# Relu and row sum of a 16384 x 1024 array on one core: two row regions (111 and 17 rows per partition) in place of three (1, 111 and 16)

## The chip, the core and the metric

The kernel runs on one core of a Trainium2 chip. The metric is device time in microseconds (us): the median of repeated executions. Beside those stands one execution recorded by the profiler, whose span runs from the first instruction to the last.

## The reference

```python
def reference(x):                      # x: (32, 512, 1024) float32
    relu_x = np.maximum(x, 0)
    return np.sum(relu_x, axis=-1).astype(np.float32)    # (32, 512)
```

There are 32 x 512 = 16384 rows of 1024 numbers; each gives one sum of its positive numbers. The input is 67.1 MB, the output 64 KB.

## The kernel before, in words

**Layout.** The 16384 rows are dealt to 128 partitions, 128 rows to each. `REGIONS = [1, 111, 16]` cuts the input into three consecutive regions; in a region of n rows per partition, partition p owns n neighbouring rows, so that a load of several rows is one run of memory per partition (n x 4 KB). The sums are collected in `res`, one column per row of the partition (128 columns).

**Big chunks.** `CHUNKS` has seven entries (`NBIG = 7`) of 16 rows per partition, 8 MB each. Chunk 0 is two loads, one row of the first region and 15 of the second; chunks 1 to 6 are one load each. They go in turn into the three slots of `buf` (`NB = 3`). All loads are issued on SP, in one queue (line 91); from chunk 3 on SP waits (line 87, semaphore `s_dve`) until VectorE (DVE) has summed the chunk that held the slot. The two loads of chunk 0 are moved ahead of SP's drain at the start of the program (line 96), so that they are issued first of all.

**Work on chunks 0 to 5.** ScalarE (ACT) applies Relu in place in steps of several rows (`ACT_STEPS`, line 145), DVE follows with `tensor_reduce` over several rows at once (`DVE_STEPS`, line 160). In chunk 5 four rows are left out of this and done whole, two by ACT (line 127: Relu with an accumulated sum) and two by DVE (line 130: maximum with 0, accumulated). After chunk 1 DVE transposes the first 32 columns of `res` into `turned` (line 169, 32 x 32 blocks), so that the sums of the one-row region lie along 4 partitions, 32 in each.

**Chunk 6 and the tail.** The rows of chunk 6 are done whole and singly, by DVE and ACT in turn. The third region is loaded in shrinking pieces: 8, 4 and 2 rows (`TAIL`, line 101), each shared half and half, and the last two rows in column pieces (line 112): columns 0 to 912 of the first of them, then the last 512 of the second, then 256 to 512 of the second; the 112 + 256 columns in between go to `seam` (line 115). Each column piece gives a partial sum into a spare column of `seam`; at last ACT sums 114 and DVE 258 columns of `seam`, partial sums among them, and so the last two rows' sums are complete. The whole tail lies in slot `tb` = 1 of `buf`; SP issues its loads once chunk 4 has been summed.

**Stores.** Three, all on SP: `turned` (4 rows of 128 bytes, line 117, after semaphore `s_turn`); the 111 columns of the second region (444 bytes per partition, line 123, after chunk 6 is summed and the last load has landed); and the 16 columns of the tail (64 bytes per partition, line 207, after the last two sums). SP then waits for all stores to land (lines 208 and 209).

Of the kernel before, what the change touches and what calls it, by code (L numbers as in the profile page):

```python
# [3 lines left out]
P = 128  # L4
D = 1024
BIG = 16
NB = 3
REGIONS = [1, 111, 16]
CHUNKS = [[(0, 0, 1), (1, 0, 15)]] + [[(1, 16 * c + 15, 16)] for c in range(6)]
ACT_STEPS = [[16], [7, 9], [7, 9], [7, 9], [4, 5, 7], [3, 4, 5]]  # L10
DVE_STEPS = [[4, 5, 7], [7, 4, 5], [7, 4, 5], [7, 4, 5], [4, 5, 7], [3, 4, 5]]
TAIL = [8, 4, 2]
CUT = 912
HEAD = 256

# [1 line left out]
def bass_relu_sum_kernel(  # L17
    nc: bass.Bass,
    x: bass.AP,
    out: bass.AP,  # L20
):

    fp32 = mybir.dt.float32
    ALU = mybir.AluOpType
    AF = mybir.ActivationFunctionType
    X = mybir.AxisListType.X

    B, S, _ = x.shape
    J = B * S // P
    NBIG = len(CHUNKS)
    assert BIG * NBIG + sum(TAIL) + 2 == J == sum(REGIONS)  # L40

    xr = x.rearrange("b s d -> (b s) d")
    of = out.rearrange("b s -> (b s)")
    start = [sum(REGIONS[:i]) for i in range(len(REGIONS))]
    xv = [
        xr[P * s : P * (s + n), :].rearrange("(p j) d -> p j d", p=P)
        for s, n in zip(start, REGIONS)
    ]
    ov = [of[P * s : P * (s + n)].rearrange("(p j) -> p j", p=P) for s, n in zip(start, REGIONS)]

    buf = nc.alloc_sbuf_tensor("buf", [P, NB, BIG, D], fp32)
    w = D - CUT
    seam = nc.alloc_sbuf_tensor("seam", [P, 2 + w + HEAD + 2], fp32)
    res = nc.alloc_sbuf_tensor("res", [P, J], fp32)
    turned = nc.alloc_sbuf_tensor("turned", [P, 32], fp32)

    n_in = NBIG + len(TAIL) + 3
    s_in = [nc.alloc_semaphore(f"s_in{i}") for i in range(n_in)]
    s_act = nc.alloc_semaphore("s_act")
    s_dve = nc.alloc_semaphore("s_dve")  # L60
    s_fact = nc.alloc_semaphore("s_fact")
    s_fdve = nc.alloc_semaphore("s_fdve")
    s_half = nc.alloc_semaphore("s_half")
    s_seam = nc.alloc_semaphore("s_seam")
    s_last = nc.alloc_semaphore("s_last")
    s_turn = nc.alloc_semaphore("s_turn")
    s_store = nc.alloc_semaphore("s_store")
    s_out = nc.alloc_semaphore("s_out")

    sp, act, dve = nc.sync, nc.scalar, nc.vector  # L70

    NTWO = len(ACT_STEPS)
    done = [sum(map(len, DVE_STEPS[: c + 1])) for c in range(NTWO)]


    tb = NBIG % NB


    code = nc.main_func.blocks[0].instructions
    arrival = next(  # L80
        i
        for i, ins in enumerate(code)
        if ins.engine == mybir.EngineType.SP and type(ins).__name__ == "InstDrain"
    )
    for c in range(NBIG + 1):
        if c >= NB:
            sp.wait_ge(s_dve, done[c - NB])
        if c < NBIG:
            i = 0
            for g, j, n in CHUNKS[c]:  # L90
                sp.dma_start(  # L91
                    out=buf[:, c % NB, i : i + n, :], in_=xv[g][:, j : j + n, :]
                ).then_inc(s_in[c], 16)
                i += n
                if c == 0:
                    code.insert(arrival, code.pop())
                    arrival += 1
    r = 0
    tail = []
    for i, n in enumerate(TAIL):  # L100
        sp.dma_start(out=buf[:, tb, r : r + n, :], in_=xv[-1][:, r : r + n, :]).then_inc(  # L101
            s_in[NBIG + i], 16
        )
        tail.append((r, n, s_in[NBIG + i]))
        r += n


    rows = xv[-1].rearrange("p j d -> p (j d)")[:, r * D : (r + 2) * D]
    flat = buf[:, tb, r : r + 2, :].rearrange("p j d -> p (j d)")
    first, second, third = [(0, CUT), (D + D // 2, 2 * D), (D + HEAD, D + D // 2)]  # L110
    for k, (lo, hi) in enumerate((first, second, third)):
        sp.dma_start(out=flat[:, lo:hi], in_=rows[:, lo:hi]).then_inc(  # L112
            s_in[NBIG + len(TAIL) + k], 16
        )
    sp.dma_start(out=seam[:, 2 : 2 + w + HEAD], in_=rows[:, CUT : D + HEAD]).then_inc(s_seam, 16)
    sp.wait_ge(s_turn, 1)
    sp.dma_start(
        out=of[0:P].rearrange("(k q) -> k q", q=32), in_=turned[0:P:32, 0:32]
    ).then_inc(s_store, 16)
    sp.wait_ge(s_fact, 1)  # L120
    sp.wait_ge(s_fdve, 1)
    sp.wait_ge(s_in[-1], 16)
    sp.dma_start(out=ov[1][:, :], in_=res[:, start[1] : start[2]]).then_inc(s_store, 16)


    def on_act(t, acc):
        return act.activation(t, t, AF.Relu, accum_out=acc)  # L127

    def on_dve(t, acc):
        return dve.tensor_scalar(  # L130
            out=t, in0=t, scalar1=0.0, scalar2=None, op0=ALU.max, op1=ALU.add, accum_out=acc
        )

    def row(c, i):
        return buf[:, c % NB, i, :], res[:, c * BIG + i : c * BIG + i + 1]

    k = 0
    for c in range(NTWO):
        alone = BIG - sum(ACT_STEPS[c])
        act.wait_ge(s_in[c], 16 * len(CHUNKS[c]))  # L140
        r = 0
        ready = []
        for n in ACT_STEPS[c]:
            t = buf[:, c % NB, r : r + n, :]
            act.activation(t, t, AF.Relu).then_inc(s_act, 1)  # L145
            k += 1
            ready += [k] * n
            r += n
        for i in range(BIG - alone // 2, BIG):
            on_act(*row(c, i))  # L150
        if alone:
            dve.wait_ge(s_in[c], 16 * len(CHUNKS[c]))
            for i in range(BIG - alone, BIG - alone // 2):
                on_dve(*row(c, i))
        r = seen = 0
        for n in DVE_STEPS[c]:
            if ready[r + n - 1] > seen:
                seen = ready[r + n - 1]
                dve.wait_ge(s_act, seen)
            dve.tensor_reduce(  # L160
                out=res[:, c * BIG + r : c * BIG + r + n],
                in_=buf[:, c % NB, r : r + n, :],
                axis=X,
                op=ALU.add,
            ).then_inc(s_dve, 1)
            r += n
        if c == 1:
            dve.wait_ge(s_dve, done[c])
            dve.transpose(out=turned[:, :], in_=res[:, 0:32]).then_inc(s_turn, 1)  # L169


    j0 = NBIG * BIG
    for c in range(NTWO, NBIG):
        act.wait_ge(s_in[c], 16 * len(CHUNKS[c]))
        dve.wait_ge(s_in[c], 16 * len(CHUNKS[c]))
        for i in range(BIG):
            ins = (on_act if i % 2 else on_dve)(*row(c, i))
            if i >= BIG - 2:
                ins.then_inc(s_fact if i % 2 else s_fdve, 1)
    for r, n, s in tail:  # L180
        act.wait_ge(s, 16)
        dve.wait_ge(s, 16)
        for i in range(r, r + n):
            f = on_act if (i - r) % 2 else on_dve
            f(buf[:, tb, i, :], res[:, j0 + i : j0 + i + 1])

    lo, hi = first
    act.wait_ge(s_in[-3], 16)
    dve.wait_ge(s_in[-3], 16)
    on_act(flat[:, lo : CUT // 2], seam[:, 0:1]).then_inc(s_half, 1)  # L190
    on_dve(flat[:, CUT // 2 : hi], seam[:, 1:2]).then_inc(s_half, 1)
    k = 2 + w
    lo, hi = second
    act.wait_ge(s_in[-2], 16)
    on_act(flat[:, lo:hi], seam[:, k + HEAD : k + HEAD + 1]).then_inc(s_seam, 1)
    lo, hi = third
    dve.wait_ge(s_in[-1], 16)
    on_dve(flat[:, lo:hi], seam[:, k + HEAD + 1 : k + HEAD + 2]).then_inc(s_seam, 1)
    act.wait_ge(s_seam, 16 + 2)
    act.wait_ge(s_half, 2)  # L200
    on_act(seam[:, 0:k], res[:, J - 2 : J - 1]).then_inc(s_last, 1)
    dve.wait_ge(s_seam, 16 + 2)
    on_dve(seam[:, k : k + HEAD + 2], res[:, J - 1 : J]).then_inc(s_last, 1)


    sp.wait_ge(s_last, 2)
    sp.dma_start(out=ov[-1][:, :], in_=res[:, start[-1] : J]).then_inc(s_out, 16)
    sp.wait_ge(s_store, 16 * (len(REGIONS) - 1))
    sp.wait_ge(s_out, 16)
# [28 lines left out]
```

## Time and profile before

| | us |
|---|---|
| median of 3 runs | 160.85 (160.80 to 160.91) |
| span of the profiled execution, first to last instruction | 159.4 |
| what the median has beyond that span | 1.45 |
| DVE busy in the span | 120.6 |
| ACT busy in the span | 101.5 |

The profiled execution's own time is not recorded apart from its span, so the span stands for it. In the lines shown further down, a line of the timeline reads: start, duration, engine, source line, operation, what it writes and reads, how many instructions were merged, and in brackets the time that the engine sat idle ahead of it and what ended that. A line of the chain reads: start, duration, engine or DMA, tile and line. "SPq" is SP's queue; its durations are those of issuing.

### The profile page before, as it was taken

How to read it: one execution, taken by the hardware profiler on the slowest of the kernel's cores; microseconds unless marked ns; L12 is line 12 of the kernel's file. 1: busy time of each engine (PE TensorE's matmuls, PEld its weight loads, DVE VectorE, ACT ScalarE, POOL GpSimd, SP SyncE). 2: the span in 40 equal slices, each digit the busy share in tenths (PEclk: the TensorE clock that was granted, in tenths of full speed). 3: DMA queues.
4: the chain of work that ended last, by engine and by line, in shares of the span. 5: the costliest groups of instructions: out<-in, count | busy, mean ns of one | idle time of the engine just before them, and what ended most of it. 6: DMA issues, size and time to landing. Idle time of an engine off the chain costs nothing.

```text
span 159.4 us, 150 instructions
## 1 busy us (share of the span) xinstructions
DVE 120.6 (76%) x59; ACT 101.5 (64%) x54; POOL 0.2 (0%) x4
## 2 busy tenths in 40 slices
DVE  0000000009999999999999999999999999898995
ACT  3000059980799708996099941999329980496975
POOL 0000000000000000000000000000000000000000
DMA  9997996996996997989979969969969979798994
GB/s 378 493 401 339 493 526 263 526 526 263 526 493 296 526 444 345 526 378 411 526 312 477 526 263 526 526 263 526 526 263 526 444 345 526 321 469 374 417 400 142
DMA packets 2457, 67.18 MB, mean 421 GB/s; under 512 B 536, under 2 KB 792, under 8 KB 1176
## 3 DMA queue, kind: packets, MB, share of 16 engines
q1 hardware_dynamic: 2456, 67.18, 98.1%
q14 instruction: 1, 0.01, 0.0%
HBM read 67.11 MB, written 0.07 MB: 421 GB/s over the span
## 4 chain that ended last, share of the span: by engine, by line
DVE 55%; DMA 34%; ACT 9%; SPq 2%; issue 0%
DVE res L160 54%; DMA buf<-in_x_dram 34%; ACT buf L145 9%; SPq L101 1%; SPq L112 1%; DVE buf L130 0%; DVE seam L130 0%; SPq L91 0%; DVE turned L169 0%
## 5 line engine op out<-in xcount | busy, mean ns | idle before, releaser
L160 DVE TENSOR_REDUCE res<-buf 128x4 f32<-128x4096 f32 (+3 forms) x18 | 99.4, 5596 | 35.5 <-ACT buf L145 35.5
L145 ACT ACTIVATE buf<-buf 128x7168 f32<-128x7168 f32 (+5 forms) x13 | 80.4, 6233 | 46.1 <-DMA buf<-in_x_dram 46.1
L127 ACT ACTIVATE buf<-buf 128x1024 f32<-128x1024 f32 (+2 forms) x19 | 19.0, 999 | 8.9 <-DMA buf<-in_x_dram 8.9
L130 DVE TENSOR_SCALAR_CACHE_REDUCE buf<-buf 128x1024 f32<-128x1024 f32 (+2 forms) x19 | 20.7, 1143 | 1.7 <-DMA buf<-in_x_dram 1.6
L127 ACT ACTIVATION_READ_ACCUMULATOR buf<-buf 128x1 f32 x19 | 3.6, 188 | 0.0
L145 ACT ACT_TABLE_LOAD x1 | 1.3, 1283 | 1.3 <-PEq L223 1.3
L130 DVE DVE_READ_ACCUMULATOR buf<-buf 128x1 f32 x19 | 1.6, 84 | 0.0
L130 DVE TENSOR_SCALAR_CACHE_REDUCE seam<-seam 128x258 f32<-128x258 f32 x1 | 0.4, 421 | 0.0
L127 ACT ACTIVATE seam<-seam 128x114 f32<-128x114 f32 x1 | 0.3, 300 | 0.1
L169 DVE STREAM_TRANSPOSE turned<-res 128x32 f32<-128x32 f32 x1 | 0.2, 211 | 0.0
L127 ACT ACTIVATION_READ_ACCUMULATOR seam<-seam 128x1 f32 x1 | 0.2, 186 | 0.0
L223 POOL MEMSET const-bfloat16-1.0<- 128x1 bf16 x1 | 0.1, 101 | 0.0
L223 POOL MEMSET const-uint8-127<- 128x1 uint8 x1 | 0.1, 101 | 0.0
L223 POOL MEMSET const-float32-0.0<- 128x1 f32 x1 | 0.1, 98 | 0.2 <-issue 0.2
L223 POOL MEMSET const-float32-1.0<- 128x1 f32 x1 | 0.1, 98 | 0.0
L130 DVE DVE_READ_ACCUMULATOR seam<-seam 128x1 f32 x1 | 0.1, 82 | 0.0
## 6 DMA issues: line engine op xcount, KB each, us to landing
buf<-in_x_dram SPq DMA_DIRECT2D x1, 7680.0 KB, 21.1
buf<-in_x_dram SPq DMA_DIRECT2D x1, 4096.0 KB, 25.3
buf<-in_x_dram SPq DMA_DIRECT2D x1, 2048.0 KB, 29.9
buf<-in_x_dram SPq DMA_DIRECT2D x1, 1024.0 KB, 31.9
buf<-in_x_dram SPq DMA_DIRECT2D x1, 512.0 KB, 3.3
buf<-in_x_dram SPq DMA_DIRECT2D x1, 456.0 KB, 32.5
buf<-in_x_dram SPq DMA_DIRECT2D x1, 256.0 KB, 32.7
seam<-in_x_dram SPq DMA_DIRECT2D x1, 184.0 KB, 32.6
```

Of the source, the lines that this page charges most:

```text
L101: sp.dma_start(out=buf[:, tb, r : r + n, :], in_=xv[-1][:, r : r + n, :]).then_inc(s_in[NBIG + i], 16)
L112: sp.dma_start(out=flat[:, lo:hi], in_=rows[:, lo:hi]).then_inc(s_in[NBIG + len(TAIL) + k], 16)
L127: return act.activation(t, t, AF.Relu, accum_out=acc)
L130: return dve.tensor_scalar(out=t, in0=t, scalar1=0.0, scalar2=None, op0=ALU.max, op1=ALU.add, accum_out=acc)
L145: act.activation(t, t, AF.Relu).then_inc(s_act, 1)
L160: dve.tensor_reduce(out=res[:, c * BIG + r : c * BIG + r + n], in_=buf[:, c % NB, r : r + n, :], axis=X, op=ALU.add,).then_inc(s_dve, 1)
L169: dve.transpose(out=turned[:, :], in_=res[:, 0:32]).then_inc(s_turn, 1)
L223: nc = _bacc.Bacc("TRN2", target_bir_lowering=False, num_devices=1)
```

## The change

The input is cut into two regions of 111 and 17 rows per partition. Chunk 0 is one load of 15 rows; the row that the one-row region held comes in through the tail, whose first piece is 9 rows instead of 8. In that piece ACT now takes five rows and DVE four. The transpose on DVE, its tile, its semaphore and its store are gone. The last store has 17 columns (68 bytes per partition) instead of 16. The last two rows are loaded into a tile of their own, `ends`, as the tail slot's 16 rows would no longer hold 17 rows. Chunk 0's ACT step has 15 rows and its last DVE step 6 instead of 7; the columns of `res` shift with it (`col`).

```diff
-REGIONS = [1, 111, 16]
-CHUNKS = [[(0, 0, 1), (1, 0, 15)]] + [[(1, 16 * c + 15, 16)] for c in range(6)]
-ACT_STEPS = [[16], [7, 9], [7, 9], [7, 9], [4, 5, 7], [3, 4, 5]]
-DVE_STEPS = [[4, 5, 7], [7, 4, 5], [7, 4, 5], [7, 4, 5], [4, 5, 7], [3, 4, 5]]
-TAIL = [8, 4, 2]
+REGIONS = [111, 17]
+CHUNKS = [[(0, 15)]] + [[(16 * c + 15, 16)] for c in range(6)]
+ACT_STEPS = [[15], [7, 9], [7, 9], [7, 9], [4, 5, 7], [3, 4, 5]]
+DVE_STEPS = [[4, 5, 6], [7, 4, 5], [7, 4, 5], [7, 4, 5], [4, 5, 7], [3, 4, 5]]
+TAIL = [9, 4, 2]
...
-    turned = nc.alloc_sbuf_tensor("turned", [P, 32], fp32)
+    ends = nc.alloc_sbuf_tensor("ends", [P, 2 * D], fp32)
...
-            for g, j, n in CHUNKS[c]:
+            for j, n in CHUNKS[c]:
                 sp.dma_start(
-                    out=buf[:, c % NB, i : i + n, :], in_=xv[g][:, j : j + n, :]
+                    out=buf[:, c % NB, i : i + n, :], in_=xv[0][:, j : j + n, :]
                 ).then_inc(s_in[c], 16)
...
-    flat = buf[:, tb, r : r + 2, :].rearrange("p j d -> p (j d)")
+    flat = ends[:, :]
...
-    sp.wait_ge(s_turn, 1)
-    sp.dma_start(
-        out=of[0:P].rearrange("(k q) -> k q", q=32), in_=turned[0:P:32, 0:32]
-    ).then_inc(s_store, 16)
     sp.wait_ge(s_fact, 1)
     sp.wait_ge(s_fdve, 1)
     sp.wait_ge(s_in[-1], 16)
-    sp.dma_start(out=ov[1][:, :], in_=res[:, start[1] : start[2]]).then_inc(s_store, 16)
+    sp.dma_start(out=ov[0][:, :], in_=res[:, 0 : start[1]]).then_inc(s_store, 16)
...
-        if c == 1:
-            dve.wait_ge(s_dve, done[c])
-            dve.transpose(out=turned[:, :], in_=res[:, 0:32]).then_inc(s_turn, 1)
...
-            f = on_act if (i - r) % 2 else on_dve
+            f = on_act if (i - r + n) % 2 else on_dve
```

## The prediction

> **What bounds the kernel now.** I read the page first, for the load of each engine and of the DMA queue; then the chain of waits; then the timeline, for the times at which pieces of the input land.
>
> ```profile
> DVE 120.6 (76%) x59; ACT 101.5 (64%) x54; POOL 0.2 (0%) x4
> ...
> q1 hardware_dynamic: 2456, 67.18, 98.1%
> ...
> buf<-in_x_dram SPq DMA_DIRECT2D x1, 7680.0 KB, 21.1
> ...
> buf<-in_x_dram SPq DMA_DIRECT2D x1, 512.0 KB, 3.3
> ...
> out_dram<-res SPq DMA_DIRECT2D x1, 8.0 KB, 1.4
> ```
>
> No engine is full, but the DMA queue's packets take 98.1% of what 16 DMA engines have in the span. That is the bound to test.
>
> ```profile
> 35.50 34.59 DVE res L160 x6
> ...
> 70.33 51.73 DVE res L160 x9
> ...
> 124.39 32.60 DMA buf<-in_x_dram
> ...
> 157.01 0.44 DVE buf L130 x2
> ...
> 157.47 0.43 DVE seam L130 x2
> ```
>
> The chain lays 54% on DVE, which looks like a second bound. It isn't one: it enters DVE only because SP issues the tail's loads when DVE has freed a slot (122.05), and then the last load needs 32.60 us to land, because it stands in the queue behind chunk 6. The landings tell which of the two is late:
>
> ```profile
> 40.97 13.95 ACT L145 ACTIVATE buf<-buf 128x7168 f32<-128x7168 f32 x2 [5.50 <-DMA buf<-in_x_dram]
> 60.31 13.95 ACT L145 ACTIVATE buf<-buf 128x7168 f32<-128x7168 f32 x2 [5.39 <-DMA buf<-in_x_dram]
> 79.67 13.95 ACT L145 ACTIVATE buf<-buf 128x7168 f32<-128x7168 f32 x2 [5.41 <-DMA buf<-in_x_dram]
> ...
> 118.36 10.63 ACT L145 ACTIVATE buf<-buf 128x3072 f32<-128x3072 f32 x3 [5.31 <-DMA buf<-in_x_dram]
> ...
> 137.72 1.06 ACT L127 ACTIVATE buf<-buf 128x1024 f32<-128x1024 f32 x1 [6.65 <-DMA buf<-in_x_dram]
> ...
> 147.43 1.06 ACT L127 ACTIVATE buf<-buf 128x1024 f32<-128x1024 f32 x1 [1.29 <-DMA buf<-in_x_dram]
> ...
> 152.32 1.06 ACT L127 ACTIVATE buf<-buf 128x1024 f32<-128x1024 f32 x1 [0.62 <-DMA buf<-in_x_dram]
> ...
> 154.84 1.06 ACT L127 ACTIVATE buf<-buf 128x1024 f32<-128x1024 f32 x1 [0.32 <-DMA buf<-in_x_dram]
> ```
>
> ACT waits for a landing each time, and chunks land 19.35 us apart from 21.61 to 137.72 without a gap: (137.72 - 21.61) / 6. That is 1.21 us per row (0.524 MB, 433 GB/s), so DMA never stood still for want of a free slot. The span is therefore a start, 67.1 MB at this rate, and what follows the last landing (157.01 to 159.39: one 256-column sum, the seam, the last store). The median lies 1.46 us above the span of 159.39; I carry that over unchanged.
>
> **Part by part.** The bytes stay the same, so only what a packet costs beyond its bytes, the start and the end can move.
>
> *Head: one load fewer.* 16 rows take 19.35 us, and chunk 0 landed at 21.61, so 2.26 us lie ahead of it. The one-row load alone landed after 3.3, less 1.21 for its row: 2.09. The difference, 0.17 us, is my upper estimate of what having two loads costs. The packet records in the trace give the lower: a 4 KB packet takes 0.159 us, a row within a 60 KB packet 2.268/15 = 0.151, and each DMA engine has 8 of them, so 8 x 0.008 + one semaphore write of 0.01 = 0.07 us. The tail's pieces agree with something between: 8 rows landed 9.71 after chunk 6 (8 x 1.21 = 9.68, so 0.03 over), 4 rows 4.89 (0.05 over), 2 rows 2.52 (0.10 over). A piece costs the more, the smaller its packets. I take -0.12, the middle of 0.07 and 0.17. The wider bounds: 0, if those 0.1 us are the first packets' start-up and pass to the 15-row load; and -0.58, because the DMA engine that ended its one-row part last needed 1.79 us for it (1.24 to 3.03 in the packet records) where 8 x 0.151 is 1.21. The packets of chunk 0 and all later ones then run 1.2 us earlier.
>
> [...]
>
> *Tail: 9 rows instead of 8.* Row for row the same bytes in longer packets: 0 for DMA, and the piece lands when the 8-row piece did, since one row fewer lies ahead of it. The larger part is on ACT, which gets a fifth row. Its rows start every 1.04 us: 147.43, 148.49, 149.53, 150.57, 151.60; the fifth ends with its accumulator read (0.19) at 152.74. The 4-row piece landed at 152.32, so ACT is late by 0.42 where it sat idle 0.62 before. It starts at about 152.71, its two rows end at about 154.86 with the step to a new piece (0.16 from the accumulator's start, as at 155.80 to 155.96), and the 2-row piece landed at 154.84. So ACT is 0.02 late, and its cover (0.62 + 0.32 idle) is used up. From there ACT runs without a gap to 157.38, and the next thing, the seam sum at 157.47, waits for DVE's 256-column sum (ends 157.44). That is some 0.09 of cover more. I take 0; bounds 0 and +0.10 (1.04 less 0.94). DVE keeps four rows, so nothing there.
>
> *Pitch of the tail in memory,* 68 KB per partition instead of 64 KB: the 8-row piece moved at 432 GB/s and the chunks, with their other pitch, at 433. Nothing is lost now that another pitch could give back: 0.
>
> *The transposed store goes.* DVE's transpose (0.21 us at 70.11) and the wait ahead of it save DVE time that is no bound: DVE still waited 0.42 us for chunk 6. Its DMA issue (0.63 us on SP at 125.35) is followed by a 31.0 us wait of SP at line 122. Its four packets take 0.013 us each and run after the loads of their DMA engines (156.62 and later). 0; bounds 0 and -0.02.
>
> *Slots.* With one row less in chunk 0 the first landing is at about 20.4, ACT's step 13.86 x 15/16 = 13.0 instead of 13.86, DVE's last step there a seventh shorter (7.6 to 6.5). DVE frees slot 0 about 1.2 + 0.9 + 1.1 = 3.2 us earlier than 52.86, while chunk 2, whose load covers the wait, lands 1.2 earlier than 60.31. The cover grows from 7.45 to 9.4. Nothing is added; `ends` needs no slot at all.
>
> *The last store* has 68 bytes per partition instead of 64, and these no longer begin at multiples of 64 bytes in the output. A 64-byte packet takes 0.011 us and a 128-byte one 0.013, which gives 8 x 0.002 = 0.02 per DMA engine. The 444-byte store, laid as unevenly, took 1.26 us from its issue to its last packet's end, the 64-byte one 1.13. Bounds 0 and +0.13; I take +0.02, because 68 is nearest to 64.
>
> [...]
>
> **Sum** on the profiled execution: -0.12 + 0 + 0 + 0.02 = -0.10, a span of 159.29 instead of 159.39; and a median of 160.75.
>
> **Rivals.** About 0.2% (0.32 us) is what a measurement of this kernel can tell from no change.
>
> *A: the start-up moves instead of going.* The first packet of the earliest DMA engines took 0.620 us instead of 0.159: a latency of the first read, not of small packets. If the 15-row load pays all of it, the head saves 0 and the store's 0.02 remains: 160.87. For it: the 0.620. Against it: 4 KB packets are dearer per row even in steady flow. Chance 22%.
>
> *B: the head saves much more.* In the records half of the DMA engines lost a further 0.1 to 0.2 us on their small packets at about 2.1 us. If the small packets caused that, the slowest engine gains up to 0.58: 160.85 - 0.58 + 0.02 = 160.29. [...] Chance 14%, spread from 160.53 down to 160.29.
>
> *C, slower: ACT's odd row reaches the end.* The fifth row has almost exactly the cover it needs. If the 9-row piece lands later against its followers, ACT is late by as much. A piece's arrival is spread over 0.48 us between DMA engines (146.62 to 147.10); were that lost, ACT would be 0.02 + 0.48 late, less 0.09 of cover at the seam: +0.41, with the sum above 160.75 + 0.41 = 161.16. It decides from 0.07 us of lateness of the 9-row piece on (0.02 + 0.07 = 0.09), and passes 0.2% at about 0.5 us. With no cover at all the row would cost 1.04: 161.79. Against it: the spread stays with the same DMA engines from piece to piece, so the spacing holds. Chance 10%, from 161.17 on.
>
> *That it doesn't do what it says* can only be A here: the order of the loads and the bytes are fixed by the code.
>
> **How the numbers follow.** Forecast 54%, A 22%, B 14%, C 10%. The forecast and A lie within 0.2%: same 76%; B is faster, 14%; C is slower, 10%. The range leaves out the far parts of B and C, about 10% on each side: 160.4 to 161.1. It takes in the head's 0 to -0.4 and the bounds of the store and of ACT together (+0.13 + 0.10, from 160.85).
>
> **What would show it.** Right: the first landing at 20.3 to 20.4; the 9-row piece at about 147.3 and the last load at about 156.9; ACT without idle time ahead of the 4-row piece and almost none ahead of the 2-row one; the seam sums starting together; last store 1.4 us to landing. A: the last load lands at 157.0 as before. C: ACT still in its column pieces when DVE stands ready for the seam. Wrong altogether: a chunk pitch other than 19.35, which would mean that memory layout matters where I gave it 0, or a last store of clearly more than 1.5 us.

## The result, and the profile after

The changed kernel takes 161.84 us (161.63 to 161.94, 5 runs) against 160.85 us; the ratio is 1.006, 95% interval 1.0048 to 1.0072. It is slower by 0.99 us where 0.10 less was forecast, and outside the range. The profiled execution took 161.88, with a span of 160.196.

The page of the changed kernel, its DMA lines, and its list of DMA issues (the last column is us from issue to landing):

```profile
q1 hardware_dynamic: 2304, 67.18, 97.7%
...
buf<-in_x_dram SPq DMA_DIRECT2D x1, 7680.0 KB, 21.1
...
out_dram<-res SPq DMA_DIRECT2D x1, 8.5 KB, 1.6
```

The 15-row load takes 21.1 us from its issue, as before, though the one-row load no longer stands ahead of it in the queue. The last store takes 1.6 instead of 1.4. The timeline says what that does to the landings:

```profile
21.12 13.00 ACT L143 ACTIVATE buf<-buf 128x15360 f32<-128x15360 f32 x1 [19.06 <-DMA buf<-in_x_dram]
40.46 13.95 ACT L143 ACTIVATE buf<-buf 128x7168 f32<-128x7168 f32 x2 [6.34 <-DMA buf<-in_x_dram]
59.81 13.95 ACT L143 ACTIVATE buf<-buf 128x7168 f32<-128x7168 f32 x2 [5.40 <-DMA buf<-in_x_dram]
...
137.21 1.06 ACT L124 ACTIVATE buf<-buf 128x1024 f32<-128x1024 f32 x1 [6.64 <-DMA buf<-in_x_dram]
...
148.13 1.06 ACT L124 ACTIVATE buf<-buf 128x1024 f32<-128x1024 f32 x1 [2.50 <-DMA buf<-in_x_dram]
...
157.66 0.42 DVE L127 TENSOR_SCALAR_CACHE_REDUCE ends<-ends 128x256 f32<-128x256 f32 x1 [0.37 <-DMA ends<-in_x_dram]
...
158.13 0.30 ACT L124 ACTIVATE seam<-seam 128x114 f32<-128x114 f32 x1
158.13 0.42 DVE L127 TENSOR_SCALAR_CACHE_REDUCE seam<-seam 128x258 f32<-128x258 f32 x1
...
158.59 0.34 SPq L202 DMA_DIRECT2D out_dram<-res  x1
```

In the kernel before, the first landing and the last store's issue were:

```profile
21.61 13.86 ACT L145 ACTIVATE buf<-buf 128x16384 f32<-128x16384 f32 x1 [19.06 <-DMA buf<-in_x_dram]
...
157.93 0.34 SPq L207 DMA_DIRECT2D out_dram<-res  x1
```

The chunk pitch is still 19.35 us. The first landing is at 21.12, not at 20.4, and every later landing carries that delay; the last one comes at 157.66 instead of 157.01. Both seam sums start together. The loss has three places:

| us | before | changed | difference |
|---|---|---|---|
| last landing | 157.01 | 157.66 | +0.65 |
| from it to the last store's issue | 0.92 | 0.93 | +0.01 |
| from that issue to the end of the span | 1.46 | 1.61 | +0.15 |
| time beyond the span, median of executions | 1.37 (75 of them) | 1.60 (5) | +0.23 |

They add up to 1.04, against 0.99 between the medians (the profiled execution is not the median one).

### The profile page after: what moved, and what is told of

The parts are those of the page before. It is cut to its first block, busy times and chain, and to the rows that moved or that the text cites. A ratio compares the mean times of both kernels' runs of the same rounds, so it can differ in the third digit from the quotient of the medians.

```text
span 160.2 us, 149 instructions
## 1 busy us (share of the span) xinstructions
DVE 119.6 (75%) x58; ACT 101.6 (63%) x56; POOL 0.2 (0%) x4
## 3 DMA queue, kind: packets, MB, share of 16 engines
q1 hardware_dynamic: 2304, 67.18, 97.7%
## 4 chain that ended last, share of the span: by engine, by line
DMA 53%; DVE 28%; ACT 17%; SPq 1%; issue 0%
DMA buf<-in_x_dram 31%; DVE res L158 27%; DMA ends<-in_x_dram 22%; ACT buf L143 17%; SPq L102 1%; SPq L113 1%; DVE ends L127 0%; DVE seam L127 0%
## 5 line engine op out<-in xcount | busy, mean ns | idle before, releaser
L158 DVE TENSOR_REDUCE res<-buf 128x4 f32<-128x4096 f32 (+4 forms) x18 | 98.5, 5538 | 34.8 <-ACT buf L143 34.8
L143 ACT ACTIVATE buf<-buf 128x7168 f32<-128x7168 f32 (+5 forms) x13 | 79.5, 6168 | 46.9 <-DMA buf<-in_x_dram 46.9
L124 ACT ACTIVATE buf<-buf 128x1024 f32<-128x1024 f32 x18 | 18.8, 1043 | 9.1 <-DMA buf<-in_x_dram 9.1
L127 DVE TENSOR_SCALAR_CACHE_REDUCE buf<-buf 128x1024 f32<-128x1024 f32 x17 | 19.8, 1217 | 3.8 <-DMA buf<-in_x_dram 3.7
L127 DVE TENSOR_SCALAR_CACHE_REDUCE ends<-ends 128x456 f32<-128x456 f32 (+1 forms) x2 | 1.0, 522 | 0.4 <-DMA ends<-in_x_dram 0.4
L124 ACT ACTIVATE ends<-ends 128x456 f32<-128x456 f32 (+1 forms) x2 | 1.2, 606 | 0.0
## 6 DMA issues: line engine op xcount, KB each, us to landing
buf<-in_x_dram SPq DMA_DIRECT2D x1, 7680.0 KB, 21.1
```

What stands on the lines that cost most here:

```text
L127: return dve.tensor_scalar(out=t, in0=t, scalar1=0.0, scalar2=None, op0=ALU.max, op1=ALU.add, accum_out=acc)
L158: dve.tensor_reduce(out=res[:, col[c] + r : col[c] + r + n], in_=buf[:, c % NB, r : r + n, :], axis=X, op=ALU.add,).then_inc(s_dve, 1)
```

## The experiments

**First theories**, on the first landing: the length of the first packets ("size" in the expectations), their distance in memory ("address", later "pitch"), or the barrier that one load fewer lets go earlier (ACT's first instruction, its table load, began at 0.78 instead of 1.27).

*One row first, in the same region.*

```diff
-CHUNKS = [[(0, 15)]] + [[(16 * c + 15, 16)] for c in range(6)]
+CHUNKS = [[(0, 1), (1, 14)]] + [[(16 * c + 15, 16)] for c in range(6)]
```

> The changed kernel with its first load of 15 rows cut into one row and 14 rows of the same region, both ahead of the barrier. Three theories for the first landing, which came 0.72 us later than bytes alone explain (21.12 instead of 21.61 - 1.21 = 20.40). Size: a long packet as the very first read of each DMA engine is dear; then a short first packet brings the landing to about 20.4 and the median to 160.9 to 161.1, the rest being the 17-column store. Barrier: with one load ahead of the barrier the other engines start 0.49 us earlier and their table and instruction loads meet the first packets; two loads ahead put that back, so also 160.9 to 161.1. Address: the first read was contiguous over partitions in the kernel before and is strided by 444 KB in the changed one; still strided here, so 161.8.

161.72 (161.56 to 162.06). The first landing, in the timeline:

```profile
20.88 13.00 ACT L143 ACTIVATE buf<-buf 128x15360 f32<-128x15360 f32 x1 [18.35 <-DMA buf<-in_x_dram]
```

Between the theories: 0.24 earlier than in the changed kernel, 0.48 later than 20.40. In this one profile, a short first packet whose 128 runs lie 444 KB apart cures a third of the delay. The last store took 1.73 us to the end of the span, which eats half of the gain.

*Fifteen rows first, in the kernel before.*

```diff
-CHUNKS = [[(0, 0, 1), (1, 0, 15)]] + ...
+CHUNKS = [[(1, 0, 15), (0, 0, 1)]] + ...      # each still to its own place in the slot
```

> The kernel before with the two loads of chunk 0 in the other order: 15 rows of the second region first, then the one row of the first region. Tail and stores are untouched, and two loads still lie ahead of the barrier. Size: the landing of chunk 0 moves from 21.6 to about 22.3 and the median to 161.5 to 161.7. Barrier: no change, 160.85. Address: as size, 161.5 to 161.7, since the first read is now strided.

161.37 (161.31 to 161.44), ratio 1.0033 (1.0021 to 1.0045), and:

```profile
22.18 13.86 ACT L146 ACTIVATE buf<-buf 128x16384 f32<-128x16384 f32 x1 [19.63 <-DMA buf<-in_x_dram]
```

The same bytes in the same number of loads, only in the other order, land 0.57 later than 21.61. Nothing else changed, so the order of the first two loads alone costs 0.52 us of the median. The barrier theory, which expected no change here, loses (ACT's table load began at 1.27, as in the kernel before).

*The barrier earlier, in the kernel before.*

```diff
-                if c == 0:
+                if c == 0 and g == 0:      # the 15-row load is now issued behind the barrier
```

> The kernel before with only the one-row load ahead of the barrier; the 15-row load is issued after it. The other engines start about 0.5 us earlier, as in the changed kernel. Size and address: 160.85, as the 15-row load is still issued before the one row has been read (at most +0.2 if the queue runs dry for a moment). Barrier: 161.4 or more.

160.80 to 163.19, median 161.30 of 12. Three executions took 160.80 or 160.81, as fast as the kernel before, so with an early barrier the time can stay the same. In the profiled one (162.94; ACT's table load at 0.79) the first landing came at 23.93: the 15-row load was issued at 0.80 instead of 0.45, and the packet records show a DMA engine whose last 4 KB packet ended at 2.52 and whose first 60 KB packet began at 4.04.

*Regions of 112 and 16.*

```diff
-REGIONS = [111, 17]
+REGIONS = [112, 16]
-CHUNKS = [[(0, 15)]] + [[(16 * c + 15, 16)] for c in range(6)]
+CHUNKS = [[(0, 1), (1, 15)]] + [[(16 * c + 16, 16)] for c in range(6)]
-TAIL = [9, 4, 2]
+TAIL = [8, 4, 2]
...
```

> The changed kernel with regions of 112 and 16 rows, chunk 0 loaded as one row and then 15, tail of 8, 4 and 2 rows as in the kernel before, no transposed store, last store of 16 columns (64 bytes). Size: 160.75 to 160.85, since all that is left of the change is the store that was dropped; against the first kernel of this group the difference is the last store with its 17 columns and the ninth tail row, which I put at 0.1 to 0.3. Address: 161.6, the first read being strided.

161.47 (161.31 to 161.59). The first landing:

```profile
21.89 13.86 ACT L143 ACTIVATE buf<-buf 128x16384 f32<-128x16384 f32 x1 [19.36 <-DMA buf<-in_x_dram]
```

That is 0.28 later than with the contiguous row. The span is 159.7, and the last store, 64 bytes again, takes 1.49. But 1.86 us lie beyond the span: a part that I had not counted as the change's at all.

**Distance or length?**

*The kernel before, rewritten with a plain store.* Regions 1, 111, 16; instead of the transpose

```diff
+    sp.wait_ge(s_dve, done[0])
+    sp.dma_start(out=ov[0][:, :], in_=res[:, 0 : start[1]]).then_inc(s_store, 16)
```

> The regions, chunks and tail of the kernel before (1, 111, 16; one contiguous row first), written in the changed kernel: no transpose, the 128 sums of the one-row region stored straight from their column (4 bytes per partition, issued behind the loads), last two rows in their own tile. Against the fourth kernel of the first group only the pitch of the first row's read differs. Pitch (the first read is dear where its 128 runs lie 444 KB apart): first landing 21.6, span 159.4. Length alone (the pitch does not matter): landing as there, 21.9. The median is 160.8 to 160.9 if what lies outside the span is 1.4 us as in the kernel before, and 161.1 to 161.3 if the 1.6 to 1.9 us of the changed kernel and its variants come from the dropped transposed store or the tile for the last rows.

166.58 (166.39 to 167.17). The landing is at 21.67, as the distance theory had it, but the end is not. DMA issues, and SP's own waits (longest in the last column):

```profile
out_dram<-res SPq DMA_DIRECT2D x1, 0.5 KB, 36.6
out_dram<-res SPq DMA_DIRECT2D x1, 8.0 KB, 7.2
```

```profile
SPq L206 <- DMA out_dram<-res: 6.8, 1, 6.8
```

128 runs of 4 bytes, side by side in the output, hold up the stores behind them: the last needs 7.2 us instead of the 1.4 that it took behind the transposed store.

*Fifteen rows first, 60 KB apart.*

```diff
-REGIONS = [111, 17]
-CHUNKS = [[(0, 15)]] + [[(16 * c + 15, 16)] for c in range(6)]
+REGIONS = [15, 96, 17]
+CHUNKS = [[(0, 0, 15)]] + [[(1, 16 * c, 16)] for c in range(6)]
...
```

> The changed kernel with its 111 rows cut into regions of 15 and 96: the first load is 15 rows at once as there, in packets of the same 60 KB, but its 128 runs lie 60 KB apart and not 444 KB; one small store more, behind the loads. Pitch: first landing 20.4 to 20.6 instead of 21.12, median 161.1 to 161.3. Length: 21.1 and 161.8 as in the changed kernel. Both by half: 20.8 and 161.5.

161.94 (161.93 to 162.26):

```profile
21.13 13.00 ACT L145 ACTIVATE buf<-buf 128x15360 f32<-128x15360 f32 x1 [19.05 <-DMA buf<-in_x_dram]
```

The landing is that of the changed kernel to 0.01: 60 KB or 444 KB from run to run is the same. At 60 KB the runs of 60 KB lie side by side, without a gap, and that does not help: for long runs the distance theory fails.

*The changed kernel with a contiguous first row*, regions 1, 110, 17, its sums stored by 4 bytes:

> The changed kernel with regions of 1, 110 and 17: one contiguous row first, then 14 rows, the rest as in the changed kernel (tail of 9, 4 and 2 rows, 17-column last store), and the one-row region's sums stored straight from their column. Against the first kernel of the first group only the pitch of the first row's read differs. Pitch: first landing 20.4 to 20.5 instead of 20.88; the last store's issue 0.4 to 0.5 us earlier; span 159.5 to 159.65, of which 0.15 to 0.25 is the 68-byte store. Length: 20.88 and 161.7 as there.

166.82: the slow store again. The landing came at 20.51, as the distance theory had it. *The same with the last store cut in two:*

> The kernel with regions of 1, 110 and 17, its last store cut in two: the first two columns of the tail (8 bytes per partition) go with the 110 columns' store, the last 15 (60 bytes) are stored at the end. If the 17-column store is slower because its runs do not begin at multiples of 64 bytes, these 60 bytes are slower too: 1.6 to 1.75 us from the last issue to the end of the span. If it is because 68 bytes are more than 64: 1.46 to 1.48, as for the 16-column store, and the median 0.15 to 0.25 below the same kernel with 17 columns.

166.98: the store of 4-byte runs hides what was asked. Both were run again with the transposed store. *Contiguous row, 17 columns, transposed store:*

```diff
-REGIONS = [111, 17]
+REGIONS = [1, 110, 17]
-CHUNKS = [[(0, 15)]] + [[(16 * c + 15, 16)] for c in range(6)]
+CHUNKS = [[(0, 0, 1), (1, 0, 14)]] + [[(1, 16 * c + 14, 16)] for c in range(6)]
...
```

> Regions of 1, 110 and 17 in the changed kernel, one contiguous row first, with the one-row region's sums transposed and stored as in the kernel before, since 4-byte runs cost over 5 us. This undoes only the head of the change and keeps its tail and its last store. Landing 20.4 to 20.5; the last store issued at 157.95 to 158.1; 1.6 to 1.75 us from there to the end of the span, 159.6 to 159.7; with 1.6 outside a median of 161.2 to 161.3, with 1.4 of 161.0 to 161.1. So about 0.6 of the 1.0 us is given back.

161.66 (161.46 to 161.73):

```profile
20.50 13.00 ACT L149 ACTIVATE buf<-buf 128x15360 f32<-128x15360 f32 x1 [17.95 <-DMA buf<-in_x_dram]
...
158.13 0.34 SPq L211 DMA_DIRECT2D out_dram<-res  x1
```

The head is repaired: 20.50 where the same row at 444 KB landed at 20.88 and the 15-row load at 21.12. The end follows less: the last store is issued 0.46 earlier than in the changed kernel, then takes 1.73 to the end of the span, and 1.56 lie beyond. The median gains 0.18 where I expected 0.6. *And with the last store cut:*

```diff
-    sp.dma_start(out=ov[-1][:, :], in_=res[:, start[-1] : J]).then_inc(s_out, 16)
+    sp.dma_start(out=ov[-1][:, 2:], in_=res[:, start[-1] + 2 : J]).then_inc(s_out, 16)
...
```

> The same, with the last store cut in two: two columns of the tail (8 bytes per partition) just behind the 110 columns' store, and the last 15 columns (60 bytes) at the end. Uneven starts as the cause: 1.6 us or more from the last issue to the end of the span. Size as the cause: 1.46 to 1.48. The last issue itself comes about 0.4 later than in the sister kernel, for the store ahead of it in SP's queue.

161.37 (161.26 to 161.79). The last store's line in the DMA issues:

```profile
out_dram<-res SPq DMA_DIRECT2D x1, 7.5 KB, 1.7
```

60 bytes, fewer than 64, are as slow: 1.73 from the issue (158.13) to the end of the span (159.859). So size alone doesn't decide; the runs again begin 68 bytes apart. That the uneven starts do it is likely but not shown, because the store of 8-byte runs just ahead, which lie beside these runs in the output, may have a share.

**Beyond the span.**

*The kernel before with the last rows in a tile of their own:*

```diff
+    ends = nc.alloc_sbuf_tensor("ends", [P, 2 * D], fp32)
...
-    flat = buf[:, tb, r : r + 2, :].rearrange("p j d -> p (j d)")
+    flat = ends[:, :]
```

> The kernel before with the last two rows loaded into a tile of their own, nothing else changed. What lies outside the span was 1.32 to 1.41 us in all executions of kernels built on the one before, and 1.5 to 2.0 in those built on the changed one. If the tile (another place in on-chip memory, another allocation) is the cause: 1.6 outside, span 159.4, median 161.05. If it isn't: 160.85.

160.84, ratio 0.9995 (0.9986 to 1.0004): the tile costs nothing.

*Without the transpose and its store:*

```diff
-            dve.transpose(out=turned[:, :], in_=res[:, 0:32]).then_inc(s_turn, 1)
...
-    sp.dma_start(
-        out=of[0:P].rearrange("(k q) -> k q", q=32), in_=turned[0:P:32, 0:32]
-    ).then_inc(s_store, 16)
```

> The kernel before without the transpose and without its store; the first 128 sums are not written at all, so its time tells what these two operations cost and nothing else. My prediction gave them nothing on the path: span 159.4. If their absence is what lengthens the time outside the span, the median is 161.05 to 161.3; if not, 160.85.

161.41 (161.24 to 161.51), ratio 1.0028 (1.0016 to 1.0039). Less work, and slower. The spans are 159.5 to 159.7, against 159.5 in the median of the kernel before; beyond them lie 1.74 to 1.91. Its first landing serves a comparison below:

```profile
21.78 13.86 ACT L139 ACTIVATE buf<-buf 128x16384 f32<-128x16384 f32 x1 [19.24 <-DMA buf<-in_x_dram]
```

*Each of the two alone:*

> The kernel before with the transpose but without its store: the first 128 sums are not written. In the run without either, 1.74 to 1.91 us lay outside the span instead of 1.32 to 1.41. If the DVE operation's presence is what counts: 1.37 outside, median 160.85 to 160.95. If the store's: 1.8 and 161.35 to 161.45. If neither by itself (only how long each engine's program is): something in between or other.

160.80, 1.38 beyond the span.

> The kernel before without the transpose but with the store of 4 x 128 bytes, which takes its bytes from the untransposed columns, so that the first 128 outputs are not the sums. Store theory: 1.37 outside the span, 160.85 to 160.95. DVE theory: 1.8, 161.35 to 161.45.

161.31, 1.81 beyond. So it is DVE's operation, not the store. *A copy in its place:*

```diff
-            dve.transpose(out=turned[:, :], in_=res[:, 0:32]).then_inc(s_turn, 1)
+            dve.tensor_copy(out=turned[:, :], in_=res[:, 0:32]).then_inc(s_turn, 1)
...
```

> The kernel before with a plain copy of the 32 columns on DVE in place of the transpose, and without its store (the first 128 sums are not written). If only the length of DVE's program counts: 1.37 outside the span, median 160.80 to 160.90. If the transpose as an operation counts: 1.8 outside, 161.3 to 161.4.

160.82, ratio 1.0003 (0.9994 to 1.0012), 1.35 beyond: a copy does it as well as a transpose. *And the changed kernel with its odd row on DVE:*

```diff
-            f = on_act if (i - r + n) % 2 else on_dve
+            f = on_act if (i - r) % 2 else on_dve
```

> The changed kernel with the ninth tail row given to DVE instead of ACT: DVE five rows at 1.14 us, ACT four. Span: DVE ends the 9-row piece 5 x 1.14 = 5.70 after its landing where the 4-row piece follows after 4.89, and has 0.2 to 0.4 us of idle time behind it, so it reaches the last pieces some 0.2 to 0.5 late: 160.4 to 160.7. If each engine's program length sets what is outside, this differs from the 1.55 to 1.65 of the changed kernel: 1.37 or 1.8. If the dropped transpose does, it stays at 1.55 to 1.65.

161.70 (161.52 to 161.95); 1.35 beyond the span, as in the kernel before. The spans are 160.2 to 160.6, a little longer, and the timeline has the reason:

```profile
158.26 0.30 ACT L124 ACTIVATE seam<-seam 128x114 f32<-128x114 f32 x1 [0.21 <-DVE ends L127]
```

Now ACT waits for DVE at the seam; the end is about 0.13 later than with the row on ACT (158.26 instead of 158.13). So the 0.23 beyond the span goes with how the change lengthens or shortens the engines' programs. In medians: with ACT's as before and DVE's not shorter 1.35 to 1.38; with ACT's one row longer 1.56 to 1.66, with or without the operation on DVE; with DVE's one operation shorter alone 1.81 to 1.90.

One thing in the traces goes with it. The page of the kernel before counts one packet on a queue of the kind "instruction":

```profile
q14 instruction: 1, 0.01, 0.0%
```

The changed kernel's page has no such line. Its packet records have two such packets, of 8 KB each, which begin 1.32 and 1.60 us after the end of the span. This divides all twenty profiles: in the eight kernels with 1.35 to 1.38 beyond the span, one 8 KB instruction packet begins between 0.44 us ahead of the span's end and 0.06 behind it, and none later; in the other twelve, one or two begin 1.30 to 1.66 behind it. So the loss goes with an instruction packet that begins only after the kernel's last instruction; no run changes that alone, and for which engine it is the records don't say.

**The last two.** *Two loads ahead of the barrier in the changed kernel:*

```diff
-                if c == 0:
+                if c <= 1:
```

> The changed kernel with chunk 1's load moved ahead of the barrier too, so that the other engines start about 0.45 us later, as in the kernel before. Barrier theory: first landing 20.4 to 20.6, median 161.2 to 161.4. Length and distance of the first read: landing 21.0 to 21.15 and median 161.75 to 161.85, no change from the changed kernel.

161.65 (161.57 to 161.89), first landing 21.32 in the profiled execution, the slowest of the five: the barrier is as late as in the kernel before (ACT's table load at 1.25, there 1.27), and the head is not repaired. That theory is out. *Half a row first, in the kernel before:*

```diff
+                half = D // 2 if g == 0 else D
+                for lo in range(0, D, half):      # two loads of 512 columns for the first row
...
```

> The kernel before with its contiguous first row loaded as two halves (2 KB packets). If the cost of the first read grows with the packet's length all the way down, the landing comes 0.05 to 0.1 earlier than 21.61 and the median falls to 160.75 to 160.8. If only far-apart or long first reads are dear, 2 KB packets gain nothing and cost a little (8 more packets per DMA engine at about 0.01): 160.85 to 160.95.

163.07 (163.03 to 163.35), landing at 24.00. The first packets are short, but the 15-row load, now the third, is issued at 0.91 instead of 0.45, and on the 16 DMA engines the first of its packets began between 2.90 and 4.93 (2.50 to 2.94 in the kernel before). Whether the 2 KB packets or the later issue did this isn't separated. Splitting in this way doesn't help, and no version here that writes all sums is faster than the one before.

**The heads together**, from profiled executions (a landing of 15 rows is raised by 1.21 to compare):

| first read | kernel | first landing, as of 16 rows |
|---|---|---|
| 4 KB runs, side by side | before; plain store; 1, 110, 17 | 21.61; 21.67; 21.71 |
| 4 KB runs, 444 or 448 KB apart | 112 and 16; one row first | 21.89; 22.09 |
| 60 KB runs, 444 KB apart | fifteen first; changed; two loads ahead | 22.18; 22.33; 22.53 |
| 60 KB runs, 60 KB apart (side by side) | 15, 96, 17 | 22.34 |

Each landing is that of a single execution. The same first load scatters: 21.60 to 21.78 in eleven profiles with 4 KB runs side by side, and 22.33, 22.35 and 22.53 in three that begin like the changed kernel. So neighbouring rows of the table are hard to tell apart. The spans of all executions say more. These four kernels have the same tail and the same last store of 64-byte runs on multiples of 64, and apart from operations that the runs above show to cost nothing within the span, they differ by the first read:

| first read | kernel | median span |
|---|---|---|
| 4 KB runs, side by side | before; without transpose and store | 159.5; 159.6 |
| 4 KB runs, 448 KB apart | 112 and 16 | 159.6 |
| 60 KB runs, 444 KB apart | fifteen first | 160.0 |

Here long first packets cost 0.4 to 0.5; distance costs 0.1 at most. With 17 columns distance is as small: one row first has a median span of 160.1 both at 444 KB and side by side. But there the length shows little too, 160.1 against the changed kernel's 160.2; the section on the prediction comes back to this.

## Why the prediction was wrong

**What bounds the kernel:** right. The chunk pitch stayed at 19.35 us, and what was late at the head (21.12 instead of 20.40) was late at the end (157.66 instead of 157.01).

**Head, the step that failed.** It priced the dropped load at -0.12, between 0 and -0.58. The runs give +0.57 for the order of the two loads alone, and +0.65 at the last landing. I had taken the 0.17 us by which two loads exceeded one for the cost of the short load, and allowed at worst that a fixed start-up passes to the next load. But the start-up wasn't fixed in these runs: as of 16 rows, the first landing came at 21.60 to 22.09 with a first read of 4 KB runs and at 22.18 to 22.53 with 60 KB runs. The packet records show where: in the kernel before, all 16 DMA engines began between 1.01 and 1.37 and ended their first row by 2.94. In the changed kernel their first 60 KB packets took 2.59 to 3.55 us (later ones 2.27), and one engine began only at 1.91. Fourteen engines had their 15 rows by 20.21, the last two at 20.51 and 20.75, and the load counts as landed only when the last engine is done (its last semaphore update came at 21.10, ACT started at 21.12). In the packet records, joined end to start, no engine of the changed kernel pauses for more than 0.01 us up to the 9-row piece, and the two stay behind: the 9-row piece arrived from 146.63 to 147.65, a spread of 1.02 instead of 0.48. The short first load in the kernel before makes the start of the stream cheaper (0.57 us at the first landing), and I had read it as an expense. That a long first read is dear was shown, by the order of the two loads alone; that distance is dear was not. Why the first long packets take so long, 2.59 to 3.55 us against 2.27, no run shows.

Rival A was the nearest, with its 0.620 us of latency in the first packets; but it let the head at worst save nothing. No case allowed that the replacement pays more.

**Last store:** the step was mis-sized, and priced in the wrong place. I took 0.02 of a bound of 0.13, because 68 is nearest to 64 in size. Ten profiles with 64-byte runs on multiples of 64 have 1.46 to 1.49 from the last issue to the end, six with 68 bytes 1.61 to 1.74, and 60 bytes uneven 1.73: +0.15 here, up to 0.27 elsewhere. The prediction's own sign of being wrong, a last store of clearly more than 1.5 us to landing, showed at 1.6. Both my figures came from packets, but the packets hardly changed: their records end 1.04 us after the issue with 64 bytes and 1.05 with 68. The time is lost behind them, from the last packet's end to the landing: 0.38 to 0.41 with 64 bytes, 0.51 to 0.64 with 68. So that the 444-byte store's 0.13 comes near the 0.15 is luck: its packets themselves are longer (22 to 29 ns against 8 to 11). (The prediction's packet times count from 0.09 us ahead of the span's start; its 1.26 and 1.13 are 1.17 and 1.04 on the timeline, and the difference stays.) The 0.02 that I had worked out from the times of the 64- and 128-byte packets stands against 0.15 to 0.27 measured. What cost least were 64-byte runs on multiples of 64 (1.46 to 1.49), and 4-byte runs side by side held up the next store by 5.7 us (7.2 less 1.5). Why, no run shows.

**"I carry that over unchanged":** wrong, 1.60 instead of 1.37 beyond the span. Within the span I was right that transpose and store cost nothing (159.6 without, 159.5 with). What an instruction does to the time beyond the span no view of one kernel could show; the copy in its place and the odd row moved to DVE do. The late instruction packets are the only sign in the traces of what happens there; the cause is open.

**Tail, ACT's odd row:** right. ACT was 0.32 late for the 4-row piece (153.03, 153.35) where I gave 0.42. It had no idle time ahead of the 4-row and the 2-row piece, and the seam sums started together; the 9-row piece took 148.13 - 137.21 = 10.92, and 9 x 1.21 is 10.89. C did not happen: the whole stream was late, not one piece against the others. **Pitch of the tail** and **tile:** nothing, right. **Slots:** right; slot 0 was free at 50.46 and chunk 2 landed at 59.81, a cover of 9.35 where I gave 9.4.

**What stays open:** how much of the 0.99 is the head's. The order of the loads alone is worth 0.52 of the median, and the contiguous first row put back into the changed kernel gave back 0.47 with the cut store. With 17 columns it gave back only 0.18, though 0.62 at the first landing and 0.45 at the last; a slower store in the profiled execution (1.73 against 1.61) and a scatter of about 0.2 between executions of these kernels take the rest, and I can't separate them.

## What to carry to other kernels

In this kernel, bound by a DMA stream that keeps its engines busy for 98.1% of the span (97.7% in the changed one), what the slowest DMA engine lost at the start was still lost at the end (+0.65 us at the last landing): in a kernel like it, look at how long the packets of the first read are before removing a small load ahead of a big one. Price a store by its landing, not by its bytes or packets alone: here the last store took 1.46 to 1.49 us to the end of the span with 64-byte runs on multiples of 64, and 1.61 to 1.74 with 68- or 60-byte runs 68 bytes apart. Avoid 4-byte runs at the end of a kernel, where they made the last store take 7.2 us. And before you carry the time beyond the span over, remember that it is not a constant: here one tiny instruction moved it by 0.44 us.

## What the runs showed of the hardware that I had not expected

- A store of 128 runs of 4 bytes side by side made the store behind it land 5.7 us later (7.2 us after its issue instead of 1.4 to 1.5).
- Two stores whose packets end alike (1.04 and 1.05 us after the issue) landed 0.15 us apart (1.46 and 1.61): the cost of the 68-byte runs showed only behind the last packet.
- Leaving out a small instruction (0.2 us on DVE) lengthened the whole by 0.46 us, nearly all of it outside the span: 160.85 with it, 161.31 without; beyond the span 1.37 and 1.81. The twelve kernels here with 1.56 or more beyond the span have 8 KB instruction packets that begin 1.30 to 1.66 us after its end, the other eight have none there.
- A load issued 0.80 to 0.91 us after the start, behind short loads, began on single DMA engines only at 4.0 to 4.9 us in two profiled executions (162.94 and 163.03; the first of these kernels took 160.80 to 163.19).
